# A fused encoder block: the first gate pair's front issued inside the last output pair

## The chip, the cores and the metric

The kernel runs on one core of a Trainium2 chip. The metric is the device time of one execution in microseconds (us). Its three runs before the change have a median of 945.7 us (945.49 to 946.87). A traced execution shows every instruction of the five engines: PE (TensorE, matmuls, with its weight loads as PEld), DVE (VectorE), ACT (ScalarE), POOL (GpSimd) and SP (SyncE, which here only issues DMAs).

## What is computed

The reference is one layer of a hybrid encoder, cut here to what matters, for 512 rows of one request group and 1024 of another, 1536 rows of 1024 values in all:

```python
xn = rmsnorm(h, norm_mix_g)
z = xn @ w_in
att = diff_attention(q, k, v, lam, rel_bias)
att = rmsnorm(att, subln_g, SUBLN_EPS) * (1.0 - lambda_init)
att = att.reshape(b, s, ATT_WIDTH) * jax.nn.silu(g_att)
fno = fourier_mix(u, w_fourier) * jax.nn.silu(g_f)
h = h + jnp.concatenate([att, fno], axis=-1) @ w_out
gate = jax.nn.sigmoid(rmsnorm(h, ple_norm_g) @ w_ple_gate)
h = h + gate * (p_i @ w_ple_proj)
return rmsnorm(h, final_norm_g)
```

The change lies in the last four lines: the output projection (`w_out`), the gate (`w_ple_gate`), the small product `p_i @ w_ple_proj` and the final norm.

## The kernel before

Every float32 product is made of three matmuls: each operand is split into a high and a low part (`split`, L53: ACT copies the high part, DVE subtracts to get the low one), and high times high, high times low and low times high are added in PSUM.

The kernel goes through five stages: values and Fourier inputs, the Fourier mixing, attention with the remaining input columns as filler between its steps, the output projection, the gate. The change touches the last two, from about 668 us on.

The rows are worked on in tiles of 128. Tiles 0 and 1 are projected inside the attention stage (`project`, L671; tile 1's product is finished by `project_end`, L665). The other ten go in pairs through `project_pair` (L926), one call for t = 2, 4, 6, 8, 10: the last output pair is t = 10. A pair's product of a 256 by 1024 by 1024 shape is done by a scheme with seven block products in place of eight. `left` (L908) makes the sums of the left operand's blocks and splits them (`s1` to `s4`, in the two temporaries `f1`, `f2`); the right operand's sums `t1` to `t4` were made earlier. Each block product (`product`, L621) is 12 matmuls. Their order is 11, 21, t4, t1, t2, 22, t3, into four PSUM banks b0 to b3. Some banks are used twice: DVE adds b1 (after t1) into the row tile, and only then may 22 start in b1, likewise b0 between t2 and t3. `keep` (L655) writes a finished row tile to DRAM (`hs`) and sums its squares on ACT.

Then the gate stage reads each row tile back. `front(t)` (L997) is a generator with four steps: load two row tiles and `p` (`rows_in`, L968), scale row t and turn it by eight PE transposes (`normed`, L984; `turn`, L990), the same for row t + 1, and last the remaining sums and splits. `gate_pair` (L1068), called for t = 0, 2, ..., 10, runs the seven products with the gate's weights, the products with `w_ple_proj` (`per_layer`, L1031, six matmuls each into the two `acc` banks), and finishes the rows (`finish_half`, L1037; `finish_row`, L1047). Inside pair t it steps through `front(t + 2)`.

The gate's weights come in a loop (L1123): seven blocks, in the order 11, 21, t4, t1, t2, 22, t3, each in two loads of 512 KB into a raw tile, which ACT and DVE split into the same tiles that the output projection's weights held. The raw tiles are `raw4()` (L947): a ring of four buffers of 512 KB with the tag `hn`. The same ring holds the scaled rows `ga_` and `gb` of each front, and these live until their pair's output has been written; it also holds the two raw loads of `w_ple_proj` (L962).

The order of the instructions on each engine is not written out by hand. The program is recorded in program order, and the framework's scheduler decides from it, ahead of time, the order in each engine's queue. Each engine then takes its queue strictly in that order. All loads and stores named here are issued by SP, apart from `gfin` (the final norm's factor) and one half of the last row, which ACT issues.

Of the kernel before, what the change touches and what calls it, by code (L numbers as in the profile page):

```python
# [10 lines left out]
F32 = mybir.dt.float32  # L11
F32R = mybir.dt.float32r
AF = mybir.ActivationFunctionType
ALU = mybir.AluOpType
# [18 lines left out]
def block_kernel(ctx, tc, i, yp, ys):  # L33
# [849 lines left out]
    with ExitStack() as pcx:  # L883
# [8 lines left out]
        def tmp():  # L892
            return wo.tile([P, 512], F32, tag="tmp", name="tmp", bufs=2).rearrange("p (a b) -> p a b", b=P)
# [13 lines left out]

        def left(cl):  # L908
            c11, c12, c21, c22 = cl
            a = {n: halves(n) for n in SUMS}  # L910
            a["11"] = a["11"][0], c11
            f11, f12, f21, f22 = (c.bitcast(F32) for c in cl)
            f1, f2 = tmp(), tmp()
            split(*a["12"], f12)
            split(*a["22"], f22)
            add(f1, f21, f22)
            split(*a["s1"], f1)
            sub(f2, f1, f11)
            split(*a["s2"], f2)
            sub(f2, f12, f2)  # L920
            split(*a["s4"], f2)
            sub(f1, f11, f21)
            split(*a["s3"], f1)
            return a, split_own(*a["11"])

        def project_pair(t, a, x):  # L926
            (xa, xb), L, R = x, slice(0, 512), slice(512, 1024)
# [5 lines left out]
            product(b3, a["22"], wb["t4"], True)  # L933
            sub(xb[:, L], xb[:, L], b3)
            product(b1, a["s1"], wb["t1"], True)
            add(xb[:, R], b1, xb[:, R])
            product(b0, a["s2"], wb["t2"], False)
            add(xa[:, R], b0, xa[:, R])
            product(b1, a["s4"], wb["22"], False)
            add(xa[:, R], b1, xa[:, R])  # L940
# [3 lines left out]
            for u in range(2):  # L944
                keep(t + u, x[u])

        def raw4():  # L947
            return pool.tile([P, D], F32, tag="hn", name="raw", bufs=4)

        a, (hi, lo) = left(pair_cl)  # L950
        with tc.issue_after(hi.ins), tc.issue_after(lo.ins):
            project_end(*later[0])
        for t in range(2, NT, 2):
            if t == 4:
                wp = [[pool.tile([P, D], F32R, tag=f"wp{k}{n}", name=f"wp{k}{n}") for n in "hl"]
                      for k in range(2)]
                gfin = pool.tile([P, D], F32, name="gfin")
                nc.scalar.dma_start(out=gfin, in_=i["final_norm_g"].rearrange(
                    "(a d) -> a d", a=1).broadcast_to([P, D]))
                for k in range(2):  # L960
                    raw = raw4()
                    nc.sync.dma_start(out=raw, in_=i["w_ple_proj"][0][k * P:(k + 1) * P, :])  # L962
                    split(*wp[k], raw)
            if t > 2:
                a, _ = left(load_cl(t, True))
            project_pair(t, a, [load_x(t, row(t)), load_x(t + 1, row(t + 1))])

# [29 lines left out]
        def front(t):  # L997
# [15 lines left out]
            gb = normed(t + 1, xb)  # L1013
            bank = tr if t else acc
            nc.scalar.copy(out=f21, in_=turn(gb, 0, bank()))
            ps = turn(gb, 1, bank())
            split(*a["22"], ps)
# [29 lines left out]
        def finish_row(t, u, x, g, ss, n):  # L1047
# [5 lines left out]
            for z in range(2):  # L1053
                w = slice(512 * z, 512 * z + 512)
                dst = yp[0, t * P:(t + 1) * P, w] if t < 4 else ys[0, (t - 4) * P:(t - 3) * P, w]
                if not last:
                    nc.vector.scalar_tensor_tensor(out=g[:, w], in0=x[:, w], scalar=rs, in1=gfin[:, w],
                                                   op0=ALU.mult, op1=ALU.mult)
                    nc.sync.dma_start(out=dst, in_=g[:, w])
                elif z == 0:  # L1060
                    nc.scalar.mul(out=g[:, w], in_=x[:, w], mul=rs)
                    nc.scalar.dma_start(out=dst, in_=g[:, w])
                else:
                    nc.vector.tensor_scalar(out=g[:, w], in0=x[:, w], scalar1=rs, scalar2=None,
                                            op0=ALU.mult)
                    nc.sync.dma_start(out=dst, in_=g[:, w])

        def gate_pair(t, x, p, g, a):  # L1068
# [37 lines left out]
            else:  # L1106

                xb = x[1]
                nc.vector.tensor_tensor(out=xb[:, R], in0=xb[:, R], in1=gfin[:, R], op=ALU.mult)
                for n in range(2):  # L1110
# [4 lines left out]
                    finish_half(1, 0, x, pp, g, ss[:, (4, 6)[n]:(5, 7)[n]], n)  # L1115
                    nc.vector.tensor_tensor(out=xb[:, w], in0=xb[:, w], in1=gfin[:, w], op=ALU.mult)
            finish_row(t, 1, x, g, ss, 3 if last else 2)
            return next(ahead, None)


        first = front(0)
        next(first)
        for n, tag in (("11", "x*00"), ("21", "x*10"), ("t4", "t4*"), ("t1", "t1*"), ("t2", "x*01"),  # L1123
                       ("22", "x*11"), ("t3", "t3*")):
            if n == "t4":
                *_, nxt = first
            w = wblock(n, tag)
# [93 lines left out]
```

## Time and profile before

| | |
|---|---|
| median of 3 runs | 945.7 us (945.49 to 946.87) |
| the profiled execution's own time | 947.0 us |
| its span, first to last instruction | 944.9 us |
| PE busy | 903.0 us, 96% of the span |
| PEld busy | 741.7 us, 78% |
| DVE busy | 677.8 us, 72% |
| ACT busy | 480.3 us, 51% |
| POOL busy | 93.8 us, 10% |
| 668 to 686 us (first output pair): PE busy of 18.0 | 14.70 us, DMA engines busy 0.98 |
| 768 to 797 us (end of the last output pair, gate pair 0): PE busy of 29.0 | 25.85 us, DMA engines busy 0.66 |
| 922 to 945 us (end of the last gate pair, last row): PE busy of 23.0 | 13.33 us |

The span is what the trace shows; the execution's own time is 2.1 us longer, and the profiled execution is 1.3 us longer than the median. Busy time of an engine is the time in which at least one of its instructions ran. A row of the timeline gives the start, the length, the engine, the source line, the operation, and what it writes and reads; in brackets stands how long the engine had been idle before it and what ended that idle time.

### The profile page before, as it was taken

What the parts mean: (1) busy time and instruction counts of PE and PEld (TensorE: products, weight loads), DVE (VectorE), ACT (ScalarE), POOL (GpSimd) and SP (SyncE); (2) the same over time, 40 slices, a digit from 0 to 9 for tenths busy, and PEclk for the clock granted to TensorE, in tenths of its full rate; (3) what the DMA queues carried; (4) which work ended last, traced back from release to release, by engine and by line L of the source; (5) the groups of instructions that cost most, each with busy time, mean ns of one, the idle gap of its engine ahead of it and who ended that gap; (6) DMA issues with size and microseconds to landing.
All of it is one profiled execution on the core that took longest, in us unless ns stands there. A gap on an engine that the chain in (4) does not pass through costs nothing.

```text
span 944.9 us, 13060 instructions
## 1 busy us (share of the span) xinstructions
PE 903.0 (96%) x4476; PEld 741.7 (78%) x4476; DVE 677.8 (72%) x1303; ACT 480.3 (51%) x947; POOL 93.8 (10%) x112
## 2 busy tenths in 40 slices
PE   7999999799999999999999999989999999999995
PEld 6878887578887788888888788778678877888885
DVE  7944888466853698678785986994586778767774
ACT  8833455232333566465564655663434467556552
POOL 0100000200000101101112222431000000000000
PEclk9999999989999999999999999999999999999999
DMA  8459648964536944672659548639985463233301
GB/s 309 148 178 321 237 179 312 347 215 144 157 124 208 243 126 145 159 227 80 186 171 249 171 135 247 214 109 322 346 284 167 156 214 132 101 100 101 101 30 60
DMA packets 125313, 176.14 MB, mean 186 GB/s; under 512 B 9464, under 2 KB 77304, under 8 KB 124224
## 3 DMA queue, kind: packets, MB, share of 16 engines
q1 hardware_dynamic: 123136, 171.25, 56.6%
q0 software_dynamic: 1392, 2.63, 1.1%
q10 hardware_dynamic: 720, 1.44, 0.5%
q8 instruction: 35, 0.57, 0.3%
q14 instruction: 30, 0.25, 0.1%
HBM read 115.48 MB, written 59.80 MB: 186 GB/s over the span
## 4 chain that ended last, share of the span: by engine, by line
PE 75%; DVE 10%; DMA 7%; ACT 3%; issue 2%; POOL 1%; SPq 1%; POOLq 0%; DVEq 0%; ACTq 0%
PE acc L138 22%; PE bank L624 15%; PE sc L760 6%; PE acc L66 5%; PE acc L68 5%; PE acc L67 5%; PE tr L787 3%; PE sc L66 2%; PE sc L67 2%; PE sc L68 2%; DMA raw<-sg 2%; PE tr L66 2%; PE tr L67 2%; DMA raw<-w_in 2%; PE tr L68 2%
## 5 line engine op out<-in xcount | busy, mean ns | idle before, releaser
L138 PE MATMUL acc<-xh,wch 128*128 128x512 f32 x384 | 153.3, 399 | 10.2 <-ACT wch L55 8.9
L138 PE MATMUL acc<-xl,wch 128*128 128x512 f32 x384 | 153.4, 400 | 0.0
L138 PE MATMUL acc<-xh,wcl 128*128 128x512 f32 x384 | 152.7, 398 | 0.0
L766 ACT ACTIVATE pt<-pt,mx 128x1024 f32<-128x1024 f32 (+1 forms) x96 | 96.5, 1007 | 60.5 <-DVE mx L763 58.7
L763 DVE CUSTOM_DVE_ANT_0 pt<-sc,tb 128x1024 f32<-128x1024 f32 (+1 forms) x96 | 97.8, 1040 | 20.0 <-PE sc L760 15.6
L138 PEld LDWEIGHTS acc<-xh,wch 128*128 128x128 f32 x384 | 72.8, 190 | 24.5 <-ACT wch L55 9.3
L138 PEld LDWEIGHTS acc<-xh,wcl 128*128 128x128 f32 x384 | 72.8, 190 | 14.5 <-DVE wcl L59 0.8
L138 PEld LDWEIGHTS acc<-xl,wch 128*128 128x128 f32 x384 | 72.9, 190 | 13.3 <-issue 0.2
L760 PE MATMUL sc<-kk,qq 128*128 128x512 f32 x160 | 65.5, 409 | 1.7 <-DMA qq<-qs_p 1.7
L760 PE MATMUL sc<-kll,qq 128*128 128x512 f32 x160 | 63.8, 399 | 0.0
L55 ACT CAST wth<-tr 128x512 fp32r<-128x512 f32 x80 | 45.5, 582 | 31.4 <-PE tr L787 31.3
L59 DVE TENSOR_TENSOR wtl<-tr,wth 128x512 fp32r<-128x512 f32 x80 | 53.4, 685 | 6.1 <-ACT wth L55 5.8
L782 DVE SCALAR_TENSOR_TENSOR pt<-pt,rc,pt 128x1024 f32<-128x1024 f32 (+1 forms) x48 | 54.4, 1133 | 1.1
L787 PE MATMUL tr<-ident,pt 128*128 128x128 f32 x320 | 48.4, 276 | 6.1 <-DVE g L832 4.1
L808 POOL TENSOR_TENSOR g<-ot,g 128x256 f32<-128x256 f32 x24 | 20.3, 847 | 308.0 <-ACT ot L807 301.6
L66 PE MATMUL acc<-wn,xh 128*128 128x512 f32 x128 | 50.6, 397 | 0.0
L68 PE MATMUL acc<-wn,xl 128*128 128x512 f32 x128 | 50.5, 394 | 0.0
L787 PEld LDWEIGHTS tr<-ident,pt 128*128 128x128 f32 x320 | 36.6, 140 | 17.4 <-DVE g L832 6.4
L67 PE MATMUL acc<-wn,xh 128*128 128x512 f32 x128 | 50.2, 392 | 0.0
L66 PE MATMUL tr<-wth,v 128*128 128x256 f32 x160 | 45.7, 286 | 0.2 <-DVE wtl L59 0.2
L67 PE MATMUL tr<-wtl,v 128*128 128x256 f32 x160 | 45.5, 285 | 0.2 <-DVE wtl L59 0.2
L68 PE MATMUL tr<-wth,v 128*128 128x256 f32 x160 | 45.2, 282 | 0.0
(326 smaller groups left out, 2194.0 us busy)
## 6 DMA issues: line engine op xcount, KB each, us to landing
raw<-w_in SPq DMA_DIRECT2D x29, 512.0 KB, 4.8
sot<-o SPq DMA_DIRECT2D x16, 512.0 KB, 3.6
hs<-x SPq DMA_DIRECT2D x12, 512.0 KB, 4.8
x<-hs SPq DMA_DIRECT2D x12, 512.0 KB, 3.9
xs<-x_cols SPq DMA_DIRECT2D x11, 512.0 KB, 5.9
cl<-cT SPq DMA_DIRECT2D x22, 256.0 KB, 4.1
wr<-w_out SPq DMA_DIRECT2D x8, 512.0 KB, 5.2
wr<-w_ple_gate SPq DMA_DIRECT2D x8, 512.0 KB, 5.0
```

The source lines that it names most:

```text
L55: a = nc.scalar.copy(out=hi, in_=src)
L59: return a, eng.tensor_tensor(out=lo, in0=src, in1=hi.bitcast(F32), op=ALU.subtract)
L66: nc.tensor.matmul(out=out, lhsT=wh, rhs=xh, start=start, stop=False)
L67: nc.tensor.matmul(out=out, lhsT=wh, rhs=xl, start=False, stop=False)
L68: nc.tensor.matmul(out=out, lhsT=wl, rhs=xh, start=False, stop=stop)
L138: nc.tensor.matmul(out=ps, lhsT=a[:, k], rhs=b[c][k // 4][:, k % 4], start=(n == 0), stop=(n == 23))
L624: nc.tensor.matmul(out=out[:, w], lhsT=a[u][:, k], rhs=b[v][:, k, w], start=(start and k == 0 and n == 0), stop=(k == 3 and n == 2), skip_ ...
L760: nc.tensor.matmul(out=pss[c][:, n:n + 512], lhsT=qq[c], rhs=k[c][:, n:n + 512], start=(m == 0), stop=(m == 1))
L763: nc.vector.tensor_tensor_reduce(out=pt[c][:, :T], in0=ps[:, :T], in1=tb[:, off:off + T], scale=-1.0, scalar=3e38, op0=ALU.add, op1=ALU.mi ...
L766: nc.scalar.activation(out=pt[c][:, :T], in_=pt[c][:, :T], func=AF.Exp, scale=-1.0, bias=mx[:, c:c + 1], accum_out=sm[:, c:c + 1])
L782: nc.vector.scalar_tensor_tensor(out=pt[0][:, :T], in0=pt[1][:, :T], scalar=rc[:, 1:2], in1=pt[0][:, :T], op0=ALU.mult, op1=ALU.add)
L787: nc.tensor.transpose(out=ps[:, j * P:(j + 1) * P], in_=pt[0][:, (b + j) * P:(b + j + 1) * P], identity=ident)
```

## The change

There are four parts.

1. `left` takes an argument `first`. For the first output pair (t = 2), `f1` and `f2` are the two halves of one tile of the `hn` ring, in place of the two `tmp` tiles.
2. The loads and splits of `w_ple_proj` (and the load of `gfin`) stand in the program at t = 8 in place of t = 4.
3. `front(0)` is started before the last output pair's products and is stepped inside them: the turn of row 0 after the product t4, that of row 1 after t2, the rest after `keep`. Before, `front(0)` was started after the last output pair and finished between the weight blocks 21 and t4. The special choice of `acc` banks for row 1 is dropped; all turns use the `tr` banks.
4. In the last row, the left half is multiplied by `gfin` in one piece of 512 columns after both quarters are done, and the right half gets `gfin` in the final product with the row's factor. Before, both halves were multiplied ahead of it, in pieces of 512, 256 and 256 columns.

```diff
-        def left(cl):
+        def raw4():
+            return pool.tile([P, D], F32, tag="hn", name="raw", bufs=4)
+
+        def left(cl, first=False):
...
-            f1, f2 = tmp(), tmp()
+            if first:
+                f1, f2 = raw4().rearrange("p (n a b) -> n p a b", n=2, b=P)
+            else:
+                f1, f2 = tmp(), tmp()
...
-        def project_pair(t, a, x):
+        def project_pair(t, a, x, ahead=iter(())):
...
             product(b3, a["22"], wb["t4"], True)
             sub(xb[:, L], xb[:, L], b3)
+            next(ahead, None)
             product(b1, a["s1"], wb["t1"], True)
             add(xb[:, R], b1, xb[:, R])
             product(b0, a["s2"], wb["t2"], False)
             add(xa[:, R], b0, xa[:, R])
+            next(ahead, None)
             product(b1, a["s4"], wb["22"], False)
...
             for u in range(2):
                 keep(t + u, x[u])
+            return next(ahead, None)
...
-            bank = tr if t else acc
-            nc.scalar.copy(out=f21, in_=turn(gb, 0, bank()))
-            ps = turn(gb, 1, bank())
+            nc.scalar.copy(out=f21, in_=turn(gb, 0, tr()))
+            ps = turn(gb, 1, tr())
...
-                if not last:
+                if not last or z:
                     nc.vector.scalar_tensor_tensor(out=g[:, w], in0=x[:, w], scalar=rs, in1=gfin[:, w],
                                                    op0=ALU.mult, op1=ALU.mult)
                     nc.sync.dma_start(out=dst, in_=g[:, w])
-                elif z == 0:
+                else:
                     nc.scalar.mul(out=g[:, w], in_=x[:, w], mul=rs)
                     nc.scalar.dma_start(out=dst, in_=g[:, w])
-                else:
-                    nc.vector.tensor_scalar(out=g[:, w], in0=x[:, w], scalar1=rs, scalar2=None,
-                                            op0=ALU.mult)
-                    nc.sync.dma_start(out=dst, in_=g[:, w])
...
                 xb = x[1]
-                nc.vector.tensor_tensor(out=xb[:, R], in0=xb[:, R], in1=gfin[:, R], op=ALU.mult)
                 for n in range(2):
...
-                    nc.vector.tensor_tensor(out=xb[:, w], in0=xb[:, w], in1=gfin[:, w], op=ALU.mult)
+                nc.vector.tensor_tensor(out=xb[:, L], in0=xb[:, L], in1=gfin[:, L], op=ALU.mult)
...
-        first = front(0)
-        next(first)
+        a, (hi, lo) = left(pair_cl, True)
+        with tc.issue_after(hi.ins), tc.issue_after(lo.ins):
+            project_end(*later[0])
+        for t in range(2, NT, 2):
+            if t == 8:
...
+            if t > 2:
+                a, _ = left(load_cl(t, True))
+            x = [load_x(t, row(t)), load_x(t + 1, row(t + 1))]
+            first = front(0) if t == NT - 2 else iter(())
+            next(first, None)
+            nxt = project_pair(t, a, x, first)
...
         for n, tag in (("11", "x*00"), ("21", "x*10"), ("t4", "t4*"), ("t1", "t1*"), ("t2", "x*01"),
                        ("22", "x*11"), ("t3", "t3*")):
-            if n == "t4":
-                *_, nxt = first
             w = wblock(n, tag)
```

The scheduler orders the queues anew. Three places show it.

DVE at the first output pair. `g<-tr` is the last attention tile's norm, `al`, `als` and `cl<-cl` are the low parts that `left` makes, `x<-x,acc` finishes tile 1. Before:

```order
L906 TENSOR_TENSOR tmp_6721<-c3_6591 128x512
L822 SCALAR_TENSOR_TENSOR ms_6656<-ms_6656,eps_6501 128x2
L903 TENSOR_TENSOR tmp_6722<-tmp_6721,cl_6587 128x512
L832 SCALAR_TENSOR_TENSOR g_6613<-tr_6687,gs_157,g_6613 128x256
L59 TENSOR_TENSOR al12_6718<-cl_6589,ah12_6717 128x512
L59 TENSOR_TENSOR al22_6714<-c3_6591,ah22_6713 128x512
L59 TENSOR_TENSOR als1_6710<-tmp_6721,ahs1_6709 128x512
L59 TENSOR_TENSOR als2_6712<-tmp_6722,ahs2_6711 128x512
L903 TENSOR_TENSOR tmp_6721<-cl_6587,c3_6591 128x512
L903 TENSOR_TENSOR tmp_6722<-cl_6589,tmp_6722 128x512
L59 TENSOR_TENSOR cl_6587<-cl_6587,ah11_6708 128x512
L668 TENSOR_TENSOR x_6409<-x_6409,acc_6599 128x512
```

And now:

```order
L822 SCALAR_TENSOR_TENSOR ms_6656<-ms_6656,eps_6501 128x2
L832 SCALAR_TENSOR_TENSOR g_6613<-tr_6687,gs_157,g_6613 128x256
L906 TENSOR_TENSOR raw_6721<-c3_6591 128x512
L59 TENSOR_TENSOR al12_6718<-cl_6589,ah12_6717 128x512
L59 TENSOR_TENSOR al22_6714<-c3_6591,ah22_6713 128x512
L59 TENSOR_TENSOR als1_6710<-raw_6721,ahs1_6709 128x512
L903 TENSOR_TENSOR raw_6721<-raw_6721,cl_6587 128x512
L903 TENSOR_TENSOR raw_6721<-cl_6587,c3_6591 128x512
L59 TENSOR_TENSOR cl_6587<-cl_6587,ah11_6708 128x512
L59 TENSOR_TENSOR als2_6712<-raw_6721,ahs2_6711 128x512
L59 TENSOR_TENSOR als3_6716<-raw_6721,ahs3_6715 128x512
L903 TENSOR_TENSOR raw_6721<-cl_6589,raw_6721 128x512
```

All of `left` now stands behind `g<-tr`; the low part of block 11 (`cl<-cl`) is the seventh instruction behind it, as before.

SP from the end of the output pairs on. `hs<-x` are the writes of finished rows, `x<-hs` the loads of rows for the gate, `raw<-w_ple_gate` and `raw<-sg` the gate's weights. Before (the four loads for the blocks 11 and 21 stand far ahead, among the first two output pairs):

```order
L972 DMA x<-hs_132 128x1024
L657 DMA hs_141<-x 128x1024
L972 DMA x<-hs_133 128x1024
L1136 DMA raw<-sg_149 128x1024 x2
L1136 DMA raw<-sg_148 128x1024 x2
L657 DMA hs_142<-x 128x1024
L657 DMA hs_143<-x 128x1024
L1136 DMA raw<-sg_148 128x1024
L972 DMA x<-hs_134 128x1024
L972 DMA x<-hs_135 128x1024
L1136 DMA raw<-sg_148 128x1024
```

And now:

```order
L960 DMA x<-hs_132 128x1024
L657 DMA hs_141<-x 128x1024
L960 DMA x<-hs_133 128x1024
L1135 DMA raw<-w_ple_gate 128x2x512 x2
L963 DMA pr<-p_cols 128x2x256
L1135 DMA raw<-w_ple_gate 128x2x512 x2
L657 DMA hs_142<-x 128x1024
L657 DMA hs_143<-x 128x1024
L960 DMA x<-hs_134 128x1024
L1135 DMA raw<-sg_149 128x1024
L960 DMA x<-hs_135 128x1024
L1135 DMA raw<-sg_149 128x1024
```

The four loads for 11 and 21 now stand where the first four of `sg` stood, and those come behind the writes of the last output pair's rows.

DVE at the end of the last output pair, now (`x_7392` and `x_7394` are its two rows, `bank_7403` is b0, `raw_7601` and `raw_7607` are the two loads of block 21):

```order
L906 TENSOR_TENSOR x_7394<-bank_7403,x_7394 128x512 x2
L651 TENSOR_SCALAR small_6406<-small_6406 128x1
L59 TENSOR_TENSOR als2_7452<-tmp_7463,ahs2_7451 128x512
L59 TENSOR_TENSOR als4_7460<-tmp_7464,ahs4_7459 128x512
L662 TENSOR_TENSOR small_6406<-small_6406 128x1
L903 TENSOR_TENSOR c_7462<-c_7462,c_7461 128x512
L651 TENSOR_SCALAR small_6406<-small_6406 128x1
L1142 SCALAR_TENSOR_TENSOR w21l_7600<-raw_7601,gcol_158,w21h_7599 128x512 x2
L59 TENSOR_TENSOR als3_7456<-c_7462,ahs3_7455 128x512
L1142 SCALAR_TENSOR_TENSOR w21l_7600<-raw_7607,gcol_158,w21h_7599 128x512 x2
```

Before, the splits of block 21 (`w21l`) stood between the reads of b2 and b1 of the last output pair, ahead of its last adds; now they stand behind the last add and behind L662, which waits for the squares of the last row.

## Rows read from the trace of the kernel before

**Rows 1.** The page, part 1: busy time, share of the span, instructions.

```profile
PE 903.0 (96%) x4476; PEld 741.7 (78%) x4476; DVE 677.8 (72%) x1303; ACT 480.3 (51%) x947; POOL 93.8 (10%) x112
```

**Rows 2.** Timeline of PE from 664 us: every wait over 0.2 us until the end.

```profile
669.66 0.50 PE L624 MATMUL bank<-w21h,al 128*128 128x512 f32 x1 [0.85 <-DVE al L59]
...
673.27 0.50 PE L624 MATMUL bank<-w11h,cl 128*128 128x512 f32 x1 [1.25 <-DVE cl L59]
...
686.36 0.47 PE L624 MATMUL bank<-w22h,ahs 128*128 128x512 f32 x1 [1.56 <-DVE x L906]
...
772.25 1.27 PE L993 MATMUL acc<-ident,raw 128*128 128x128 f32 x8 [1.71 <-ACT acc L660]
...
795.16 1.09 PE L993 MATMUL tr<-ident,raw 128*128 128x128 f32 x8 [1.44 <-ACT raw L986]
```

**Rows 3.** Timeline of DVE, first output pair.

```profile
667.92 0.69 DVE L903 TENSOR_TENSOR tmp<-tmp,cl 128x512 f32<-128x512 f32 x1 [4.34 <-PE acc L67]
668.53 0.48 DVE L832 SCALAR_TENSOR_TENSOR g<-tr,gs,g 128x256 f32<-128x256 f32 x1
...
672.54 0.68 DVE L59 TENSOR_TENSOR cl<-cl,ah 128x512 fp32r<-128x512 f32 x1
...
681.29 1.23 DVE L59 TENSOR_TENSOR wp0l<-raw,wp0h 128x1024 fp32r<-128x1024 f32 x1 [2.54 <-ACT wp0h L55]
...
685.53 0.68 DVE L906 TENSOR_TENSOR x<-bank,x 128x512 f32<-128x512 f32 x1
```

**Rows 4.** Timeline of SP's DMA issues, first output pair.

```profile
670.93 1.36 SPq L962 DMA_DIRECT2D raw<-w_ple_proj  x2
...
676.01 4.38 SPq L637 DMA_DIRECT2D cl<-cT  x4
```

**Rows 5.** Timeline of PE: last output pair's start, its end, gate pair 2's first product.

```profile
750.13 0.40 PE L624 MATMUL bank<-w11h,ah 128*128 128x512 f32 x1
...
769.51 1.03 PE L993 MATMUL tr<-ident,raw 128*128 128x128 f32 x8
...
801.78 0.40 PE L624 MATMUL bank<-w11h,ah 128*128 128x512 f32 x1
```

**Rows 6.** Timeline of SP's DMA issues, last output pair.

```profile
756.47 0.32 SPq L972 DMA_DIRECT2D x<-hs  x1
760.02 8.60 SPq L1136 DMA_DIRECT2D raw<-sg  x4
768.90 2.65 SPq L657 DMA_DIRECT2D hs<-x  x2
```

**Rows 7.** Timeline of DVE and ACT: weight splits.

```profile
753.87 2.74 DVE L1143 SCALAR_TENSOR_TENSOR w11l<-raw,gcol,w11h 128x512 fp32r<-128x512 f32 x4
...
763.87 1.05 ACT L55 CAST wt4h<-raw 128x1024 fp32r<-128x1024 f32 x1 [2.77 <-DMA raw<-sg]
...
764.96 1.22 DVE L59 TENSOR_TENSOR wt4l<-raw,wt4h 128x1024 fp32r<-128x1024 f32 x1
```

**Rows 8.** Timeline of DVE and ACT: last weight block, scaled row 2.

```profile
792.65 1.23 DVE L59 TENSOR_TENSOR wt3l<-raw,wt3h 128x1024 fp32r<-128x1024 f32 x1 [1.81 <-ACT wt3h L55]
...
793.96 1.15 ACT L986 ACTIVATE raw<-x,small 128x1024 f32<-128x1024 f32 x1 [0.86 <-issue]
...
796.08 1.23 DVE L59 TENSOR_TENSOR wt3l<-raw,wt3h 128x1024 fp32r<-128x1024 f32 x1 [1.61 <-ACT wt3h L55]
```

**Rows 9.** Timeline of ACT and DVE: last row.

```profile
936.82 0.42 ACT L1042 ACTIVATE raw<-raw 128x256 f32<-128x256 f32 x1
...
937.04 0.68 DVE L1109 TENSOR_TENSOR x<-x,gfin 128x512 f32<-128x512 f32 x1
...
939.30 0.42 DVE L1116 TENSOR_TENSOR x<-x,gfin 128x256 f32<-128x256 f32 x1 [0.57 <-ACT raw L1045]
...
940.70 0.72 ACT L1061 ACTIVATE raw<-x,rs 128x512 f32<-128x512 f32 x1 [1.43 <-POOL rs L653]
```

**Rows 10.** Stages: us, busy PE, PEld, DVE, ACT, POOL, granted clock, DMA share, GB/s.

```profile
934.00:945.00 11.00, 1.33 (x12) 1.13 (x10) 5.38 (x14) 3.63 (x10) 0.54 (x1) 0.79 0.20 74
```

More of the change, by code (lines that the diff above doesn't have):

```diff
@@ L945, in project_pair @@
                 keep(t + u, x[u])
[L947 to L966, printed above, removed]
+            return next(ahead, None)
         def rows_in(t):
@@ L1115, in gate_pair @@
                     finish_half(1, 0, x, pp, g, ss[:, (4, 6)[n]:(5, 7)[n]], n)
-                    nc.vector.tensor_tensor(out=xb[:, w], in0=xb[:, w], in1=gfin[:, w], op=ALU.mult)
+                nc.vector.tensor_tensor(out=xb[:, L], in0=xb[:, L], in1=gfin[:, L], op=ALU.mult)
             finish_row(t, 1, x, g, ss, 3 if last else 2)
             return next(ahead, None)
-        first = front(0)
-        next(first)
+        a, (hi, lo) = left(pair_cl, True)
[3 more added lines that the diff above has]
+            if t == 8:
+                wp = [[pool.tile([P, D], F32R, tag=f"wp{k}{n}", name=f"wp{k}{n}") for n in "hl"]
+                      for k in range(2)]
+                gfin = pool.tile([P, D], F32, name="gfin")
+                nc.scalar.dma_start(out=gfin, in_=i["final_norm_g"].rearrange(
+                    "(a d) -> a d", a=1).broadcast_to([P, D]))
+                for k in range(2):
+                    raw = raw4()
+                    nc.sync.dma_start(out=raw, in_=i["w_ple_proj"][0][k * P:(k + 1) * P, :])
+                    split(*wp[k], raw)
+            if t > 2:
[4 more added lines that the diff above has]
+            nxt = project_pair(t, a, x, first)
         for n, tag in (("11", "x*00"), ("21", "x*10"), ("t4", "t4*"), ("t1", "t1*"), ("t2", "x*01"),
                        ("22", "x*11"), ("t3", "t3*")):
-            if n == "t4":
-                *_, nxt = first
             w = wblock(n, tag)
```

## The prediction

> **What bounds the kernel now.** I read the page first: PE is busy 96% of the span [rows 1], so time can be won only where PE waits, or lost where it is made to wait. Next the timeline of PE from the output pairs on. It shows just five waits over 0.2 us before PE's work ends [rows 2]: 0.85, 1.25 and 1.56 us in the first output pair, 1.71 and 1.44 us around gate pair 0, together 6.8 us. Behind PE's last product comes the last row's tail on DVE, ACT and POOL [rows 9]. The change aims at all of these. A measurement of this kernel can tell about 0.2% (1.9 us) from no change. Last I read what sits just below PE: the chain of weight loads in gate pair 0. A raw tile is loaded, copied by ACT, subtracted by DVE, and only then is its buffer free for the next load [rows 6, 7]. Of the four buffers two hold the scaled rows of the running pair, so two serve the loads. This chain already ends late before the change: the scaled row 2, which PE waits for, starts 0.08 us after the split of block t3's first load frees its buffer (792.65 + 1.23 against 793.96) [rows 2, 8].
>
> **Part 1, the first pair's temporaries.** DVE's L903 sat idle 4.34 us until PE had finished tile 1's product, because it shared a buffer with that product's operand [rows 3]. That wait goes. But in the new order all of `left` stands behind L832, which turns the last attention tile and needs PE transposes that come after the same product. L832 ran at 668.53, directly after L903, and can be at most some 0.2 us earlier. The low part of block 11, which ends PE's 1.25 us wait, is still the seventh instruction behind L832; it started at 672.54, 4.0 us after it [rows 3]. The low part of block 12 moves one place back (0.6 us), so the 0.85 us wait grows and the second shrinks by as much. Sum: -0.1 us; the ends are 0 and -2.1 us (both waits gone). I take the low end, since the order says what is late next.
>
> **Part 2, p's weights later.** The 1.56 us wait is for DVE's read of b1 at 685.53 [rows 2, 3]. DVE takes its queue in order, and ahead of that read stood two splits of `w_ple_proj` (the first 2.54 us idle for its data) and a split of the next pair's operand, whose four loads SP could issue only from 676.01 on, behind the two 512 KB loads of `w_ple_proj` [rows 3, 4]. Now those four come first, two of them some 5 us earlier, and the read stands ahead of both splits. Ends: 0 and -1.56 us. I take -1.3, since 1 MB less stands ahead of the loads; the rest I leave for the first split, which now stands ahead of the read of b0. Parts 1 and 2 together move all that follows 1.4 us earlier.
>
> **Part 3, the front in the last output pair.** PE's 84 matmuls of that pair took 750.13 to 769.51, 0.231 us each and 2.77 us a product; turning one row takes 1.03 us [rows 5]. Two turns go in, so gate pair 0 starts at 769.5 - 1.4 + 2.0 = 770.1. The waits of 1.71 and 1.44 us in their old form are gone. Row 1 is not late for its turn: its load was issued at 756.47 [rows 6], thus now at 755.1, and with about 4 us to land and 1.15 us to scale [rows 8] it is ready near 760, 2.5 us ahead of the end of t2 at 763.5.
>
> The loads are what pays for it. Before, blocks 11 and 21 were loaded long ahead, and their buffers were free for the first t4 load at 760.02 [rows 6]. Now the scaled rows 0 and 1 take two buffers before block 11 gets any, and four loads go through the remaining two ahead of t4. I follow the first of these two.
>
> - Block 11's split on DVE now has the read of b0 in its middle, which waits for t2: 763.5 + 0.6 for the read + 0.7 for a piece (2.74 us for four [rows 7]) = 764.9. Then block 21's load is issued.
> - That load has landed by 769, but its split stands behind the pair's last adds and behind L662, which waits for the last row's squares: 770.1 + 1.2 (two adds at DVE's pace of 0.61 us for 512 columns [rows 3]) + 0.9 (squares of 512 columns with the sum's readout, an estimate between ACT's 0.42 for 256 and 1.05 for 1024 [rows 7, 9]) + 0.8 (L662 and a subtraction) + 1.4 (two pieces) = 774.4, say 774.5. Then t4 is issued, 14.5 us later than before. On SP it also stands behind the writes of rows 10 and 11 (issued from 768.90 before [rows 6]), which is no later bound.
> - One load takes 3.85 us from issue to ACT (760.02 to 763.87), 1.1 us on ACT, 1.22 us on DVE: 6.2 us [rows 6, 7]. Five (t4, t1, t2, 22, t3) end at 774.5 + 31.0 = 805.5, against 793.9 before: 11.6 us later. Before, the five took 33.9 us; DVE then also made the first front's sums, which now lie ahead. So 6.2 and 6.8 us a load are the ends, and I take 6.2.
> - Scaled row 2 and the second half of t3 follow as before, 3.4 us on (797.3 before [rows 8]): 808.9. From 797.3 PE had 4.5 us to pair 2's first product, 5.0 to its third matmul [rows 5]. Now less is left: five matmuls of t3, one of p's, two of pair 2 and the turn of row 3, 2.8 us, and some 0.5 us of waiting for row 3: 812.2 against 802.2.
>
> Part 3 ends at +10.0 us, the 1.4 us included. In between PE waits before nearly every half block, some 14 us in all, where it waited 3.15.
>
> By the Trainium skill (DMA: Bandwidth & Descriptors, Anatomy of one DMA), a transfer costs about 2.0 us plus its bytes at 436 GB/s, fitted on another issuing path: an estimate of 3.2 us for 512 KB. By it the five loads would take 3.2 us less and the time would be about 952.0; the row's 3.85 us decides.
>
> **Part 4, the last row.** The 512-wide multiplication L1109 stood in the tail at 937.04 and held back the next step until 937.65, though ACT's tanh was ready at 937.27 [rows 9]: 0.4 us. One 256-wide multiplication ahead of the last sum goes too (0.33); behind the squares a 512-wide one replaces a 256-wide one (+0.27). Sum -0.4 us. The right half's final product takes a factor more, but ACT's 0.72 us for the left half run beside it [rows 9]. Ends 0 and -0.7.
>
> **Sum.** +10.0 - 0.4 = +9.6 us. On the profiled execution (947.0 us) that is 956.6; it stood 1.3 us above the median, so I predict 955.3 us.
>
> **Rivals.**
>
> - *The loads keep up* (faster). Then only the gains are left: 1.4 + 3.15 + 0.4 = 5.0 us, 940.7 us. For it speaks that the loads of t4 to t3 held PE up only once before, for 1.44 us [rows 2]. Against it: PE would want the second half of t3 near 793, so the t4 load would have to go out near 759, as it did before; with two buffers it decides at that point. Chance 0.06.
> - *The chain starts sooner or runs quicker.* If block 21's splits are not held back, the write of row 10 bounds the t4 load: SP loads row 2 into its buffer first, after 22's read near 768 and a write as long as a load, near 772: 2.5 us less, 952.8. Chance 0.15.
> - *The loads stay as slow as before*, 6.8 us each: 3 us more, 958.3. Chance 0.14.
> - *The clock falls.* In the stretch after PE ran dry the granted clock was 0.79 [rows 10], between the levels of 2.4 and 1.2 GHz. If PE's waits in gate pair 0 bring it to the lower one, six matmuls take 2.8 us, which the two buffers' 3.1 us a load still cover; behind the last load some 2.3 us and one product of 2.8 us are added: 960.4. Chance 0.06. The Trainium skill (TensorE: Matmul & The Clock Gate, What's actually happening) says the low level is the default, released by activity; the tail's row agrees, and whether waits as short as these bring it no row here tells.
> - *No difference.* Queues that wait less than the order suggests leave gain and loss even: 945.7. Chance 0.04.
>
> **The numbers.** The forecast has 0.55. 949.5 to 960.0 takes in the two chain rivals and the ends of parts 1 and 2 (+1.4 and -2.3 around them), and leaves out the first and the last and part of the clock's. Faster 0.06, same 0.04, slower 0.90.
>
> **What would show it.** PE's timeline should show no wait for the squares (L660) before a turn, but waits for ACT and DVE splits at t4, t1, t2, 22 and t3, at each half; SP the first `sg` load 14 us later; DVE the t3 split ending near 805 and 809; the first pair's wait for b1 nearly gone, the other two still there. A t4 load before 765 would make the whole sum wrong, and so would a stretch from 770 to 810 in which PE waits under 5 us.

## The result and the profile after

The changed kernel takes 960.8 us (median of 4 runs, 958.12 to 964.32), the kernel before 946.3 beside it. The ratio is 1.0145, 95% interval 1.0122 to 1.0167; by it, as in all that follows, the changed kernel is 13.7 us slower, while the two medians lie 14.5 us apart. The forecast was 955.3 us, +9.6, with a range up to 960.0: right sign, too small a size, and the median lies just outside. The profiled execution is the quickest of the four: 958.1 us, its span 956.0 against 944.9.

The page's busy times of PE and DVE stand beside [rows 1]. DVE's work is the same; PE's extra 5 us are matmuls that ran longer:

```profile
PE 908.2 (95%) x4476; PEld 742.3 (78%) x4476; DVE 677.1 (71%) x1301; ACT 480.9 (50%) x947; POOL 95.0 (10%) x112
```

SP's DMA issues: the last two of the four loads of the next pair's operand that part 2 moves (against [rows 4]), then the last output pair (against [rows 6]). The first load of t4 (`raw<-sg`) leaves at 775.41 instead of 760.02, as the text on record had it (774.5):

```profile
675.22 1.18 SPq L637 DMA_DIRECT2D cl<-cT  x2
...
765.69 2.89 SPq L1135 DMA_DIRECT2D raw<-w_ple_gate  x2
768.82 3.58 SPq L657 DMA_DIRECT2D hs<-x  x2
...
775.41 0.32 SPq L1135 DMA_DIRECT2D raw<-sg  x1
```

DVE, against [rows 3, 7, 8]: the transposes' reader L832 with its wait (part 1), the wait for one of those four loads (part 2), block 21's split behind the sums of squares (L662), then the splits of t4 and t3. SP's first t4 load, at 775.41, leaves right behind the first half of block 21's split (773.94 + 1.40 = 775.34), which frees its buffer. The t3 split that started at 792.65 starts at 805.84:

```profile
666.75 0.48 DVE L832 SCALAR_TENSOR_TENSOR g<-tr,gs,g 128x256 f32<-128x256 f32 x1 [4.86 <-PE tr L830]
...
682.87 0.69 DVE L906 TENSOR_TENSOR tmp<-cl 128x512 f32<-128x512 f32 x1 [1.51 <-DMA cl<-cT]
...
773.21 0.15 DVE L662 TENSOR_TENSOR small<-small 128x1 f32<-128x1 f32 x1
773.94 1.40 DVE L1142 SCALAR_TENSOR_TENSOR w21l<-raw,gcol,w21h 128x512 fp32r<-128x512 f32 x2
...
781.81 1.22 DVE L59 TENSOR_TENSOR wt4l<-raw,wt4h 128x1024 fp32r<-128x1024 f32 x1 [2.08 <-ACT wt4h L55]
...
805.84 1.23 DVE L59 TENSOR_TENSOR wt3l<-raw,wt3h 128x1024 fp32r<-128x1024 f32 x1 [0.30 <-ACT wt3h L55]
...
809.28 1.23 DVE L59 TENSOR_TENSOR wt3l<-raw,wt3h 128x1024 fp32r<-128x1024 f32 x1 [0.89 <-ACT wt3h L55]
```

ACT's copies of the first halves of t4, t1 and t2, which show the step of the chain of loads:

```profile
780.74 1.04 ACT L55 CAST wt4h<-raw 128x1024 fp32r<-128x1024 f32 x1 [1.46 <-DMA raw<-sg]
...
786.98 1.05 ACT L55 CAST wt1h<-raw 128x1024 fp32r<-128x1024 f32 x1 [1.86 <-DMA raw<-sg]
...
793.02 1.05 ACT L55 CAST wt2h<-raw 128x1024 fp32r<-128x1024 f32 x1 [1.98 <-DMA raw<-sg]
```

PE's timeline, against [rows 2]. The first three waits are still there and sum to 3.63 us where they were 3.66; a fourth one is new; the two old waits around gate pair 0 are gone, and in their place, in gate pair 0 (the last output pair starts at 749.39), PE waits ahead of nearly every half block (11 rows over 0.2 us, 9.3 us together; four are shown):

```profile
668.49 0.51 PE L624 MATMUL bank<-w21h,al 128*128 128x512 f32 x1 [1.36 <-DVE al L59]
...
671.82 0.51 PE L624 MATMUL bank<-w11h,cl 128*128 128x512 f32 x1 [1.09 <-DVE cl L59]
...
685.01 0.47 PE L624 MATMUL bank<-w22h,ahs 128*128 128x512 f32 x1 [1.18 <-DVE x L906]
...
693.96 0.47 PE L624 MATMUL bank<-w21h,ah 128*128 128x512 f32 x1 [0.31 <-DVE small L651]
...
749.39 0.40 PE L624 MATMUL bank<-w11h,ah 128*128 128x512 f32 x1
...
781.83 0.79 PE L624 MATMUL bank<-wt4h,ah 128*128 128x512 f32 x1 [2.76 <-ACT wt4h L55]
783.09 0.80 PE L624 MATMUL bank<-wt4l,ah 128*128 128x512 f32 x1 [0.47 <-DVE wt4l L59]
783.68 0.63 PE L624 MATMUL bank<-wt4h,al 128*128 128x512 f32 x1
784.11 0.63 PE L624 MATMUL bank<-wt4h,ah 128*128 128x512 f32 x1
...
805.86 0.50 PE L624 MATMUL bank<-wt3h,ahs 128*128 128x512 f32 x1 [1.04 <-ACT wt3h L55]
...
807.12 0.50 PE L624 MATMUL bank<-wt3l,ahs 128*128 128x512 f32 x1 [0.76 <-DVE wt3l L59]
```

Behind the 2.76 us wait matmuls start 0.43 us apart, nearly twice the 0.23 of full pace; this half pace lasts until 788.38. The stretches (columns as in [rows 10], the granted clock third from the end, 1.00 being the level of 2.4 GHz) show it, and that it was over when t3 ran:

```profile
782.00:790.00 8.00, 7.54 (x20) 5.61 (x21) 4.70 (x5) 3.13 (x6) 0.00 (x0) 0.60 0.44 139
...
800.00:815.00 15.00, 11.92 (x55) 8.44 (x55) 10.44 (x17) 10.65 (x18) 0.54 (x1) 1.00 0.31 103
```

The last row: the right half's final product on DVE and the two last stores, before and then now. PE's last matmul starts at 935.05 before and at 946.16 now:

```profile
940.70 0.49 DVE L1064 TENSOR_SCALAR raw<-x,rs 128x512 f32<-128x512 f32 x1 [0.72 <-POOL rs L653]
941.25 0.33 SPq L1066 DMA_DIRECT2D y_sample<-raw  x1
941.45 0.37 ACTq L1062 DMA_DIRECT2D y_sample<-raw  x1
```

```profile
951.51 0.75 DVE L1044 SCALAR_TENSOR_TENSOR raw<-x,rs,gfin 128x512 f32<-128x512 f32 x1 [0.72 <-POOL rs L653]
952.26 0.39 ACTq L1049 DMA_DIRECT2D y_sample<-raw  x1
952.32 0.33 SPq L1046 DMA_DIRECT2D y_sample<-raw  x1
```

**How the traces are compared below.** Executions differ by several us in the stages ahead, which the change does not touch (the first output pair starts between 663.5 and 672.2 us), so each trace is measured in three stretches: A, from the first output pair's first product to the last output pair's first; B, from there to gate pair 4's first product; C, from the start of PE's last matmul to the span's end. The starts are the matmuls with w21 or w11 in the timeline of PE; "t4 load" and "t3 split" are the first `raw<-sg` on SP and the second split of t3 on DVE, counted from the last output pair's start.

| kernel | A | t4 load | t3 split | B | C | ratio to before (95%) |
|---|---|---|---|---|---|---|
| before | 82.0 | 9.9 | 45.9 | 78.7 | 9.85 | |
| changed | 83.0 | 26.0 | 59.9 | 90.6 | 9.84 | 1.0145 (1.0122 to 1.0167) |
| changed, again | 83.4 | 26.0 | 59.7 | 91.9 | 9.88 | 1.0154 (1.0116 to 1.0191) |
| part 3 alone | 81.8 | 26.0 | 59.9 | 92.2 | 9.81 | 1.0138 (1.0098 to 1.0178) |
| parts 1, 2, 4 | 84.0 | 9.9 | 46.5 | 79.3 | 9.89 | 1.0036 (1.0014 to 1.0058) |
| part 1 alone | 82.2 | 9.9 | 46.7 | 81.0 | 9.77 | 1.0007 (0.9992 to 1.0022) |
| part 2 alone | 82.5 | 9.9 | 47.0 | 79.8 | 9.83 | 1.0025 (1.0004 to 1.0046) |
| changed, 11 and 21 early | 84.3 | 8.7 | 48.1 | 78.8 | 9.89 | 1.0008 (0.9989 to 1.0026) |
| part 3, 11 and 21 early | 81.8 | 8.7 | 49.7 | 81.6 | 9.78 | 0.9987 (0.9964 to 1.001) |
| the same, again | 81.9 | 8.7 | 47.5 | 78.1 | 9.81 | 0.9998 (0.9981 to 1.0015) |
| part 3, only 11 early | 81.9 | 16.3 | 53.4 | 86.0 | 9.83 | 1.0061 (1.0035 to 1.0086) |
| part 3, early, loads by POOL | 86.7 | 8.9 | 51.0 | 82.3 | 10.18 | 1.0081 (1.0055 to 1.0107) |
| fill at t4 | 83.6 | 26.0 | 59.8 | 91.8 | 9.80 | 1.0152 (1.012 to 1.0185) |
| fill between | 83.4 | 26.0 | 59.2 | 90.8 | 9.87 | 1.0148 (1.0124 to 1.0172) |

### The profile page after: what moved, and what is told of

It is laid out like the page before. It is cut to its first block, busy times and chain, and to the rows that moved or that the text cites. A ratio compares the mean times of both kernels' runs of the same rounds, so it can differ in the third digit from the quotient of the medians.

```text
span 956.0 us, 13047 instructions
## 1 busy us (share of the span) xinstructions
PE 908.2 (95%) x4476; PEld 742.3 (78%) x4476; DVE 677.1 (71%) x1301; ACT 480.9 (50%) x947; POOL 95.0 (10%) x112
## 3 DMA queue, kind: packets, MB, share of 16 engines
q10 hardware_dynamic: 720, 1.44, 0.4%
## 4 chain that ended last, share of the span: by engine, by line
PE 75%; DVE 10%; DMA 8%; ACT 2%; issue 2%; POOL 1%; SPq 1%; POOLq 0%; DVEq 0%; ACTq 0%
PE acc L138 21%; PE bank L624 15%; PE sc L760 7%; PE acc L66 5%; PE acc L68 5%; PE acc L67 5%; PE tr L787 3%; PE sc L66 2%; PE sc L68 2%; PE sc L67 2%; PE tr L66 2%; PE tr L67 2%; DMA raw<-sg 2%; PE tr L68 2%; PE tr L509 1%
```

## The experiments

**The changed kernel again.**

> The changed kernel once more, beside the three others. Its four executions lay between 958.1 and 964.3 us with mean granted clocks from 0.987 down to 0.981, those of the kernel before within 2 us of each other. Theory (the chain of loads costs about 11 us every time, and the clock that falls after PE's 2.76 us wait at block t4 costs a varying rest): again 958 to 965, the longer executions with the lower clock. Rival (the four were an accident of that chip): all within 2 us.

959.48 to 961.68 us: the median is the same. From the quickest to the slowest the four have mean granted clocks of 0.988, 0.987, 0.984 and 0.982, as the theory has it; but they lie within 2.2 us of each other, so the rival is nearly right too, and the kernel before, in 13 runs on this chip, spread further (943.44 to 951.17). So the spread is no mark of the change. What this trace adds is in B, 91.9 against 90.6, though the chain of loads ends at the same place. In it the half pace came twice: at t4 as before, but shorter (783.69 to 787.10), and again behind the last load:

```profile
806.29 0.49 PE L624 MATMUL bank<-wt3h,ahs 128*128 128x512 f32 x1 [1.14 <-ACT wt3h L55]
807.55 0.80 PE L624 MATMUL bank<-wt3l,ahs 128*128 128x512 f32 x1 [0.77 <-DVE wt3l L59]
808.15 0.63 PE L624 MATMUL bank<-wt3h,als 128*128 128x512 f32 x1
```

**Part 3 alone, and everything but part 3.** The first is the kernel before with the third part of the diff, the second the changed kernel with that part undone.

> Part 3 alone, on the kernel before. Theory (part 3 makes the whole loss): 957 to 961 us, +11 to +14.5; the first load of block t4 leaves SP near 775, and PE waits for ACT and DVE splits at t4, t1, t2, 22 and t3. Rival (parts 1, 2 and 4 cost several us of it): 952 or less.

> Parts 1, 2 and 4 without part 3. By the prediction (-1.4 and -0.4): 1.8 us faster than before, about 944.5. By the reading of the trace after the change (parts 1 and 2 cost 0.9, part 4 gives 0.3): 0.6 us slower, 946.9, which is no difference. If they share part 3's loss: over 949.

Part 3 alone makes 1.0138 of the 1.0145, with the t4 load at 26.0 and the split at 59.9 again. Parts 1, 2 and 4 together are not a gain of 1.8 us: they lose 3.4 us by the time (interval 1.3 to 5.5), of which the trace shows 2.0 in A and 0.6 in B; where the rest lies is open. The median of 950.2 us falls into the third case, over 949, but not for that case's reason: the t4 load leaves at 9.9, as before the change. The two ratios together (1.0174) are more than that of the whole change, which their intervals allow.

**Part 1 and part 2 by themselves.** One is the change to `left` alone, the other this line:

```diff
-            if t == 4:
+            if t == 8:
```

> The kernel before with part 1 alone. Theory (all of the sums' work stands behind the last attention tile, so the waits only change places): PE's first two waits of the first output pair 1.36 and 1.09 us in place of 0.85 and 1.25, +0.35; the third stays near 1.5; no difference that the time shows, 945.5 to 947.5. Rival (the freed buffer takes both waits away): 2 us faster.

> The kernel before with part 2 alone. Theory (the four loads of the next pair's operand still land late, and the second load of w_ple_proj, issued behind one of them, puts its copy and its split ahead of the pair's last adds): the wait for b1 goes from 1.56 to 1.0 to 1.3 us, a new wait of 0.3 to 1.5 us stands before the second output pair's first product; 0 to 1.3 us slower, 946 to 948. The prediction's step: 1.3 us faster.

Part 1 moves the first two waits as expected (1.36 and 1.09 us). The third falls to 1.00 where about 1.5 was expected, and the time shows no difference. Part 2 takes the b1 wait from 1.56 to 1.29 and buys a new one of 0.48, ahead of the second product of the next pair, not the first; 1.0025 with an interval above 1. That is 2.4 us, more than the 0 to 1.3 expected, of which A shows 0.5. In the trace with parts 1, 2 and 4 the new wait is 1.52 us, and its cause can be followed over four engines. SP's, ACT's, DVE's and PE's rows:

```profile
690.36 0.50 SPq L1115 DMA_DIRECT2D raw<-w_ple_proj  x1
...
695.93 1.05 ACT L55 CAST wp1h<-raw 128x1024 fp32r<-128x1024 f32 x1 [3.52 <-DMA raw<-w_ple_proj]
...
698.24 1.22 DVE L59 TENSOR_TENSOR wp1l<-raw,wp1h 128x1024 fp32r<-128x1024 f32 x1
699.37 1.28 DVE L906 TENSOR_TENSOR x<-bank,x 128x512 f32<-128x512 f32 x2
...
700.80 0.47 PE L624 MATMUL bank<-w21h,ah 128*128 128x512 f32 x1 [1.52 <-DVE small L651]
```

The scheduler still issues both loads of `w_ple_proj` in the first output pair, only later: the second one stands on SP behind a load of `cl` that left only at 689.93. Its copy holds up ACT's queue for 3.52 us, its split DVE's, and behind that stand the pair's last adds, whose bank PE needs for that product (the row names L651, which follows these adds).

The trace of part 2 alone shows one thing more. In gate pair 0 PE waited 1.72 us, as it did before the change (1.71, [rows 2]), but here half pace came behind the wait, in a stretch with a granted clock of 0.86:

```profile
773.92 1.29 PE L993 MATMUL acc<-ident,raw 128*128 128x128 f32 x8 [1.72 <-ACT acc L660]
```

```profile
770.00:782.00 12.00, 10.28 (x45) 8.13 (x44) 8.62 (x16) 7.70 (x15) 1.08 (x2) 0.86 0.84 277
```

**Blocks 11 and 21 early.** The loop's body becomes a function `gate_weights`, called inside the last output pair:

```diff
             add(xa[:, L], b0, xa[:, L])
+            if t == NT - 2:
+                gate_weights("11", "x*00")
...
             add(xa[:, L], b2, xa[:, L])
+            if t == NT - 2:
+                gate_weights("21", "x*10")
```

> The changed kernel, but the loads and splits of the gate's blocks 11 and 21 stand inside the last output pair, right behind the products whose weight tiles they overwrite, and so ahead of the front's scaled rows in the ring of four buffers. The front stays where the change put it. Theory (the scaled rows took the buffers that blocks 11 and 21 needed, and the chain of loads started 15 us late): the first load of t4 leaves SP near 758 to 762, PE waits under 4 us from 770 to 815 in place of some 11, no half pace there, and pair 2 starts 10 us or more earlier: 946 to 949 with parts 1 and 2 in it. Rival (the front's turns, and the work of ACT and DVE inside the pair, cost it wherever the loads stand): 955 or more. Second rival (the last output pair itself is held up by the splits put into it): gate pair 0 starts after 773, 950 to 954.

> Part 3 alone with the same early loads of blocks 11 and 21 (parts 1, 2 and 4 undone). Theory: as the run with all parts, less the 1 to 2 us that parts 1 and 2 cost: 943 to 947, level with the kernel before or up to 3 us faster, since the waits of 1.71 and 1.44 us around gate pair 0 go and two turns of 1.03 us only change their place. Rival (the early loads do not bring the t4 load back): 955 or more.

> Part 3 alone with blocks 11 and 21 early once more, beside the kernel before in more rounds, to narrow its interval. The first time 0.9987 with an interval of 0.9964 to 1.001. Expected 0.997 to 1.000: PE's waits in gate pair 0 are 2.0 us with it and 3.15 before, and the two turns in the last output pair cost the 2 us that they cost in gate pair 0.

The whole loss goes with the order of the loads; the front is where the change put it. With all parts the ratio is 1.0008. SP and PE of that run: the t4 load is back, of the 11 waits two over 0.3 us are left, and the granted clock is 1.00 from 770 to 815.

```profile
758.82 1.64 SPq L1116 DMA_DIRECT2D raw<-sg  x2
```

```profile
794.85 0.50 PE L624 MATMUL bank<-wt3h,ahs 128*128 128x512 f32 x1 [0.95 <-ACT wt3h L55]
796.11 0.51 PE L624 MATMUL bank<-wt3l,ahs 128*128 128x512 f32 x1 [0.76 <-DVE wt3l L59]
```

Part 3 alone with the early loads is level with the kernel before (0.9998 in the longer comparison). So this is not a version that beats it: the two old waits of 1.71 and 1.44 us are gone, but the first load of t2 leaves 26.4 to 26.9 us after the last output pair's start, where it left at 22.2 before, and B is no shorter than before in any way that repeats (81.6 and 78.1).

**Only block 11 early.**

> A dose between: part 3 alone, with only block 11's loads and splits moved ahead of the scaled rows; block 21 is loaded where the change has it. In the queues block 21's four subtractions then stand between the last output pair's reads and ahead of its last adds, no longer behind the sums of squares. Theory (what sets the loss is the moment at which the t4 load goes out): t4's load at 765 to 768, between 758 (both blocks early) and 774 (none); the chain of five loads of 6.2 us then ends near 798, 2 to 5 us of the 12 are left: 948 to 952. Rival (it is a matter of all or nothing, since SP's writes of rows 10 and 11 and the loads of rows 2 and 3 hold the queue up to 775 anyway): 956 to 959 as with part 3 alone, or 946 as with both blocks early.

The t4 load at 16.3, the split at 53.4, ratio 1.0061: in between on every count. The median of 952.3 us is just above what was expected; in this trace the clock fell at t3 too (0.72 from 790 to 800). SP's rows show why the load is in between. Block 21's loads find their buffers at 751.84, but DVE splits block 21 between its reads of the running pair's banks, and t4's load waits for that split until 761.68:

```profile
751.84 0.94 SPq L1119 DMA_DIRECT2D raw<-w_ple_gate  x2
...
761.68 2.86 SPq L1119 DMA_DIRECT2D raw<-sg  x2
```

So the loss depends on the moment of the t4 load, step by step, and the "all or nothing" rival falls.

**The loads on another queue.** In part 3 with the early blocks, the line that loads the gate's weights:

```diff
-                nc.sync.dma_start(out=raw, in_=src)
+                nc.gpsimd.dma_start(out=raw, in_=src)
```

> Part 3 alone, with blocks 11 and 21 early, and all 14 loads of the gate's weights issued by POOL in place of SP. On SP the load of t2 went out 10 us after that of t1, behind the writes of rows 10 and 11 and the loads of rows 2 and 3, which wait for other things. Theory (SP's order is what is left of the chain's delay): t2's loads 1 to 4 us earlier, the waits for block t3 (1.24 and 0.75 us) gone, 944 to 946, up to 2 us faster than before. Rival 1 (the two buffers alone set the pace): as with SP's loads, 946. Rival 2 (POOL's own work, the reciprocal roots of the rows, is held up behind loads that wait for a buffer): scaled rows late, 948 or more.

A miss, 1.0081. The first load of t2 left 27.2 us after the last output pair's start (780.83), no sooner than SP's (26.4 and 26.9). DVE's and POOL's rows:

```profile
778.34 0.16 DVE L662 TENSOR_TENSOR small<-small 128x1 f32<-128x1 f32 x1
...
779.09 1.22 DVE L59 TENSOR_TENSOR wt1l<-raw,wt1h 128x1024 fp32r<-128x1024 f32 x1
...
779.25 1.46 POOL L653 TENSOR_TENSOR small<-small,mhalf 128x1 f32<-128x1 f32 x1 [2.07 <-DVE small L651]
780.83 0.57 POOL L1121 DMA_DIRECT2D raw<-sg  x1
```

The buffer for this load comes free with the split of t1's first half (779.09 + 1.22 = 780.31), and that split stands on DVE behind L662, which waits for the last row's squares. With SP's loads it is the same (split until 775.64, load at 775.72 in the first run of part 3 with early blocks). POOL's own step held the load up by 0.5 us at most. So at this place SP's order was not what bound the loads, as rival 1 has it, but the loss is not in B (82.3). It is in A, which is 4.8 us longer, with a wait of 4.03 us for b1 in the first output pair and half pace behind it (688.33 to 692.59). POOL issues two of the loads at 663.33, where SP's first left at 683.28 before; and `w_ple_proj`, whose splits stand ahead of the read of b1, reaches ACT 11.9 us after its issue (669.91 to 681.83), before 9.3 (670.93 to 680.20). That the early loads slow that one fits, but no run shows it by itself.

**The clock, twice.** In both kernels PE gets matmuls that nothing needs. In the first:

```diff
+            if t == 0:
+                product(b3, a["12"], wb["11"], True)
+                product(b3, a["12"], wb["11"], True, slice(0, 256))
             if not last:
                 product(b3, a["22"], wb["t4"], True)
```

> The changed kernel with 24 matmuls more (one product of 512 and one of 256 columns, about 4.2 us of PE) in gate pair 0 between the products 21 and t4; what they make is overwritten by t4's first matmul, so this is added work that nothing needs. They fill the 2.76 us in which PE waits for the first half of t4. Theory (that wait lets the clock fall, and the loss varies from execution to execution): matmuls of t4 and t1 0.39 us long in place of 0.63 to 0.79, executions all within 2 us of each other, at 957 to 959, though PE has 4.2 us more to do; 2 to 3 us under the changed kernel's median. Rival 1 (the clock is no part of it; the load chain alone sets the time): the same median as the changed kernel and the same spread. Rival 2 (PE itself is the bound in gate pair 0): 4 us more than the changed kernel.

The 2.76 us wait is filled and the clock is 1.00 up to 800 us, yet the time does not move: rival 1. The half pace at t4 had been free, since PE then waited for the next load anyway: the first trace of the changed kernel, which has the half pace only there, has the smallest B of those with part 3 and the late loads. But in this trace it is at t3 that the clock falls (0.89 from 800 to 815, B 91.8). The second kernel fills the waits from t1 on:

```diff
+                if fill and k % 2 == 0 and n < 2:
+                    got = b[0][:, k] if n else fill[1][1][:, 3] if k == 0 else b[1][:, 1]
+                    for _ in range(2):
+                        nc.tensor.matmul(out=fill[0], lhsT=a[0][:, 0], rhs=got, start=True, stop=True,
```

> The changed kernel with 32 matmuls of 512 columns more in gate pair 0, four per half block of t1, t2, 22 and t3: two ahead of it and two between its high and its low part, just where PE waits; they go to a bank that the next product overwrites, so this is added work that nothing needs (7.4 us at 0.231 each). In four traces of kernels with part 3 the last split of t3 starts 59.7 to 59.9 us after the last output pair's start, and from it pair 4's first product is 30.7 us away where the clock was 1.00 after 800 us, and 32.0 to 32.3 in the three where it was 0.89. Theory (the clock falls through PE's waits, and where it is low behind the last load it costs 1.3 to 1.5 us): clock 1.00 or nearly so from 790 to 815, t3's matmuls 0.39 us long, the split again at 59.7 to 59.9, pair 4 30.7 to 31.2 us behind it (part of two or four added matmuls lies behind the last split), 959 to 960, 1 us under the changed kernel. Rival (the clock falls there for another reason than PE's waits): 0.63 us a matmul for t3 in it too, 32 us, 961 to 962.

The stretch from 800 us, of the changed kernel's second trace and then of this one:

```profile
800.00:815.00 15.00, 11.93 (x46) 8.15 (x45) 9.19 (x14) 9.72 (x16) 0.31 (x1) 0.89 0.33 105
```

```profile
800.00:815.00 15.00, 13.59 (x62) 9.99 (x62) 9.63 (x15) 10.54 (x16) 0.28 (x1) 1.00 0.35 109
```

Filled, the clock stays at 1.00 from 790 us on and t3's matmuls at 0.39 to 0.40 us. B is 90.8, 1.0 to 1.4 us under the three traces whose clock fell at t3. The split came 0.6 us earlier than expected and pair 4 started 31.6 us behind it instead of 30.7 to 31.2, three added matmuls (0.7 us) being among what lies there. The whole time (median 960.6 us, ratio 1.0148) can't tell the 1 us apart. So the clock's share is read from the traces alone.

## Why the prediction was wrong in size

Stretch by stretch, in the words of the text on record:

- **Part 3 was right in mechanism and nearly in size.** Its +11.4 us (without the 1.4 of parts 1 and 2) stands against B: 78.7, 79.3, 81.0 and 79.8 in the four traces whose gate pair 0 is that of before (mean 79.7), and 90.6, 91.9 and 92.2 in the three of part 3 (mean 91.5): +11.8. Seen from the last output pair's start, the t4 load was put at 25.8 and left at 26.0; the t3 split's end was put at 60.2 and came at 61.1; pair 2's third matmul at 63.5 and 64.0 in the profiled execution. A load's step was 6.0 to 6.2 us (ACT's copies of t4, t1 and t2 at 780.74, 786.98, 793.02), as taken. Inside the sum errors partly offset each other, which is luck: the first load reached ACT 5.3 us after its issue (775.41 to 780.74), not 3.85, with row loads issued beside it, and the five took 31.7 us, not 31.0; but behind the last split PE needed 2.9 us, not 3.3. PE's waits came to 9.3 us, not "some 14"; PE was busy 5.2 us longer instead, some 3 of them at half pace (an estimate: the 13 matmuls that start from 781.83 to 787.95 would have taken 3.0 us of these 6.5 at full pace). The runs with early loads show the cause, the buffers that the scaled rows took and the place of block 21's split: with both blocks early the loss is gone, with block 11 alone early about half of it is left. No run parts these two; a ring of five buffers would.
- **Parts 1 and 2 failed: -1.4 us forecast, +1.7 us found** (A: 81.8 to 82.0 in five traces without them, the run with POOL's loads left out, 83.0 to 84.3 in six with both, means 81.9 and 83.6). The step that failed is part 2's -1.3, "since 1 MB less stands ahead of the loads". In the changed kernel's trace two of the four loads did leave some 5 us sooner, but the other two only from 675.22 on, and DVE still waited 1.51 us for one before its read of b1. So that wait fell by only 0.4, and part 1 alone lowers it by 0.6 (to 1.00). And I costed the moved loads at a rest in the b1 wait, without asking what the second split now stands ahead of: the last adds of the pair, and PE's second product of the next. In the six traces that wait is 0.3 to 1.7 us; the first output pair is 0.2 to 0.4 us longer than in the kernel before, the second 0.5 to 1.9. Part 1's -0.1 was +0.35 in the two waits, inside its sense that the order says what is late next.
- **Part 4 failed by 0.4 us.** C is 9.84 against 9.85. The step before the last was gained (the last row's final product on ACT starts 5.35 us behind PE's last matmul, before 5.65), and the left half's store leaves 0.3 us sooner (6.10 us behind that matmul, before 6.40). But the right half's product on DVE takes 0.75 us with the second factor where it took 0.49, so its store leaves no sooner (6.16, before 6.20), now last and beside the other. From the last issue to the end are 3.68 us where they were 3.45, and the gain is gone. The forecast's cover, that "ACT's 0.72 us for the left half run beside it", took no account of the stores behind; why they take longer together is not shown.
- **The sum.** +1.7, +11.8 and 0.0 make 13.5; measured 13.7. Of the 4 us that the forecast fell short, 3.1 are parts 1 and 2, 0.4 each are parts 3 and 4.
- **The rivals.** *The loads keep up* needed a t4 load near 759: it is what the early-load runs make, and there the loss is gone. *No difference* fell with the ratio. *The chain starts sooner* did not happen, nor did *the loads stay as slow* (6.0 to 6.2 us, not 6.8). *The clock falls* did, but not with its size: it counted 5.1 us behind the last load; in three of the four traces with late t4 loads and waits at t3 (the two of the changed kernel, part 3 alone, fill at t4) it was 1.2 to 1.6 (B, against 90.6), in the fourth the fall came at t4 alone, where it cost nothing that B shows. That its 960.4 lies near the median is chance. By the Trainium skill (TensorE: Matmul & The Clock Gate, What's actually happening) the low level is the default and activity releases it; the two levels, half pace behind a wait and full pace where it was filled, agree.

## What to carry to other kernels

When a step is moved earlier, list the buffers it takes and ask who was to have them: the front moved by half a stage, and four loads lost two of four buffers just ahead of a chain with no slack. Moving the loads that need those buffers along with it gave everything back, and no more. A transfer that is moved behind others takes its copy and its split along in two in-order queues, so name what stands behind them there, not only what no longer stands ahead.

## What was not expected of the hardware

- A wait of 1.71 us in gate pair 0 before the change left the clock at 1.00 (stretch from 770 to 800); the 1.72 us of the same wait with part 2 alone brought half pace (0.86). After the change the 2.76 us wait halved the pace until 788.38, and a chain of waits of 0.3 to 1.1 us did the same in other executions of the same kernel, at another place. So these traces give no length of wait that is safe. Within part 3's chain of loads a fall cost time only behind the last load.
- A load of 512 KB took 3.85 us from issue to ACT's copy before the change, 5.3 us with row loads beside it, and 6.7 us for t2 in the first run with early loads (775.72 to 782.42; 5.1 in the second, 775.01 to 780.15), which makes much of the difference between their B of 81.6 and 78.1. The rest goes with the clock, which fell at t3 in the first alone (0.87 from 790 to 800, 1.00 in the second).
